# Modulation products in groups of four, x normalised on ScalarE, and the gates' low rank taken with the first head's values

## The chip, the cores and the metric

The kernel runs on one core of a Trainium2 chip. The metric is the device time of one execution in microseconds (us). Three runs of the kernel before took 1918.33, 1924.79 and 1923.61; the median is 1923.61.

## The reference, cut to what matters

The reference is a trunk of two layers over 512 tokens of width 1024: 256 of x and 256 of ctx. A layer modulates its input (a layernorm, times 1 + scale, plus shift), projects it with `w_in` into keys and values, gated linear attention (GLA), a convolution and gates, merges the three branches, and ends with a feed-forward network (FFN) that has a modulation of its own.

```python
mod = (silu_c @ w_ada[l] + b_ada[l])[:, None, :]
sh1, sc1, g1, sh2, sc2, g2 = jnp.split(mod, 6, axis=-1)
...
def _modulate(x, shift, scale):
    return _layernorm(x) * (1.0 + scale) + shift
...
def _mem_parts(pm, p):
    k, v, kg, vg, glr = _split(pm, MEM_SPLITS)
    ...
    gf, gb = _gla_log_gates(glr, p['gla_w_a2'], p['gla_b_a'])
...
def _gla_log_gates(glr, w_a2, b_a):
    z = jnp.einsum('blnr,nrk->nblk', glr.reshape(B, L, 2, GLA_RANK), w_a2) + b_a[:, None, None, :]
    lg = jax.nn.log_sigmoid(z.astype(jnp.float32)) / GLA_TAU
```

Three things in it bear on the change: the first two sixths of the modulation (shift and scale ahead of the mixer), the normalised x of layer 0, and `glr`, the 32 columns of `w_in` (two directions by rank 16) from which the GLA gates are made.

## The kernel before, in words

**Products in three parts.** Each large product of the reference is made of three products in fp32r on TensorE: an operand is split into `hi`, its rounded part (ScalarE, line 98), and `lo`, the rest (VectorE, line 99). `mm3` (line 146) issues hi by hi, hi by lo and lo by hi. Weights come through `wload` (line 102): a tile `raw` of 1024 columns is loaded on SP's queue, split into `whi` and `wlo`, and handed on. There are five `raw`, three `whi` and two `wlo` buffers. `fm` (line 153) makes 128 output features for up to 512 tokens with one `wload` and 24 products. `tm` (line 159) makes token tiles, with the weights as the moving operand.

**Order of the work.** The program is written with the Tile scheduler: an instruction belongs to an engine, the scheduler orders each engine's instructions by priority when the program is built, and it places the waits. The engines then work through their queues in order. `tc.high_priority` moves instructions forward; `wload` uses it with `self.ahead`, which is 30 at the start and 3000 after the keys and values of layer 0. Background work is written as generators, which `step()` advances after each weight group of the main work (`self.bg` for attention and GLA, `ada` for the modulation).

**The start (`run`, line 810).** `silu_c` makes silu(c) for x and ctx as 32 columns (`self.sc`). Four token tiles of x and ctx are loaded in halves of 512 columns, their statistics taken on VectorE (line 824) and completed on GpSimd (`rstd`, lines 91 and 94), and both halves normalised in place on VectorE (line 827). Between the second and the third tile five steps of the generator `ada_head(0)` are run. `layer_consts(0)` follows: it loads the columns of constants, the query and key norms and the rotary table, and makes `rope` with four products on GpSimd (line 241). The rotary table and `rope` are two of the four `t4` tiles, and `rope` is kept.

**`ada_head` (line 254)** computes shift and scale of the mixer in four blocks j of 512 columns. A block has eight products of `self.sc` (the stationary operand, 32 columns) with 512 columns of weights, k = 0 to 7, added up in four column groups of one PSUM tile: product k writes partitions 32g to 32g + 31 with g = k % 4 (line 277). Each product appears in the trace as two records. The weights come in four loads of 1024 columns, two products each, into `t4` tiles (layer 0, even j; line 272), pairs of `qt` tiles (layer 0, odd j; line 269) or `raw` tiles (layer 1). After each load's pair of products the generator yields. After eight, the sum is copied (line 281), transposed and gathered by eight small products with `self.sel` (line 284), and added to the bias (line 285).

**Keys and values of layer 0.** `kv(start)` runs a `tm` with four weight loads. Ahead of the j-th, `start(j)` (line 935) calls `modulate` for the two 128-column units 2j and 2j + 1 of both halves of the tokens (transposes at line 344, two ScalarE instructions at line 352 and one on VectorE at 354 for each unit and half), and then advances `ada_head(0)` by five steps, the next block. Each load is followed by 24 products.

**Layer 1's modulation** is advanced by `step()` within the FFN of layer 0: five steps for each of four blocks, and then two generators `ada_gen` of nine steps (line 290; two `raw` tiles and four products in four column groups per step). The FFN's first three groups are computed in two stages of 256 tokens, the others on 512.

**GLA's low rank.** After the convolution's input, one `fm` over `wglr` (the 32 columns of glr, each direction repeated four times: 128 features) gives `pg` for 512 tokens; line 969 rounds it, and line 970 gives `glrT`, whose rows are rounded values and their rests. `gla_in(hd)` (line 976) then computes a head's keys, queries and values; the values of 256 columns come from two weight loads of 1024 columns and, for each of four token tiles, 24 products 256 wide, evacuated at line 1003. `gla_prep` (line 466), a background generator, uses `glrT` in two products per head (line 479).

Of the kernel before, what the change touches and what calls it, by code (L numbers as in the profile page):

```python
# [52 lines left out]
class Trunk:  # L53
# [48 lines left out]
    def wload(self, src, n=1024, shift=0):  # L102

        nc, tc = self.nc, self.tc
        with tc.high_priority(offset=self.ahead):
            raw = self.T("raw", [128, 1024])
            nc.sync.dma_start(out=raw[:, :n], in_=src)
            hi = self.T("whi", [128, 1152], F32R)[:, shift:shift + n]
            lo = self.T("wlo", [128, 1152], F32R)[:, shift:shift + n]
            self.split(hi, lo, raw[:, :n])  # L110
        return hi, lo

    def wload_hl(self, src):

        nc = self.nc
        with self.tc.high_priority(offset=self.ahead):
            raw = self.T("raw", [128, 1024])
            nc.sync.dma_start(out=raw, in_=src)
            his, los = [], []
            for kk in range(2):  # L120
                hi, lo = self.pair()
                self.split(hi, lo, raw[:, kk * 512:(kk + 1) * 512])
                his.append(hi)
                los.append(lo)
        return his, los
# [128 lines left out]
    def ada_head(self, l, res):  # L254
# [8 lines left out]
        for j in range(4):  # L263
            ps = self.PS("sd")
            for i in range(4):
                if l == 0 and j % 2:
                    raw = [self.T("qt", [128, 512], name="ada") for _ in range(2)]
                    for kk in range(2):
                        nc.sync.dma_start(out=raw[kk], in_=I["w_ada0"][l, j, i][:, kk * 512:(kk + 1) * 512])
                else:  # L270
                    raw = self.T("raw" if l else "t4", [128, 1024], name="ada")
                    nc.sync.dma_start(out=raw, in_=I["w_ada0"][l, j, i])
                    raw = [raw[:, :512], raw[:, 512:]]
                for kk in range(2):
                    k = 2 * i + kk
                    g = k % 4
                    nc.tensor.matmul(ps[32 * g:32 * g + 32, :], self.sc[:, k, :], raw[kk],  # L277
                                     start=(k < 4), stop=(k >= 4))
                yield
            m = self.T("cacc", [128, 512], name="m")  # L280
            nc.vector.tensor_copy(m, ps)
            tr = self.PS("tr", (128, 8))
            for t in range(4):
                nc.tensor.matmul(tr[:, 2 * t:2 * t + 2], m[:, t * 128:(t + 1) * 128], self.sel, start=True, stop=True)
            nc.vector.tensor_tensor(out=mc.rearrange("p (s h k) -> p s h k", s=2, h=2)[:, :, :, 2 * j:2 * j + 2],
                                    in0=tr.rearrange("p (h t s) -> p s h t", h=2, t=2),
                                    in1=b[:, :, :, 2 * j:2 * j + 2], op=ALU.add)
            yield

    def ada_gen(self, l, r, res):  # L290
# [3 lines left out]
        for k in range(KC):  # L294
            for hf in range(2):
                raw = self.T("raw", [128, 1024])
                c0 = (r - 1) * 2048 + hf * 1024
                nc.sync.dma_start(out=raw, in_=I["w_ada"][l, k * 128:(k + 1) * 128, c0:c0 + 1024])
# [511 lines left out]
    def run(self):  # L810
# [4 lines left out]
        self.ada0 = self.ada_head(0, mod)  # L815
        for t in range(4):
            if t == 2:
                for _ in range(5):
                    next(self.ada0)
# [5 lines left out]
            mv, rs = self.stats(st)  # L825
            for n in range(2):
                nc.vector.tensor_scalar(out=x[n], in0=x[n], scalar1=mv[:, 0:1], scalar2=rs, op0=ALU.subtract,  # L827
                                        op1=ALU.mult)
            xn[t] = x
        self.l = 0  # L830
        self.layer_consts(0)
# [17 lines left out]
    def layer(self, l, xn, mod, x0, x1, x2, mgd):  # L849
# [9 lines left out]
        ada = []  # L859
# [75 lines left out]
        def start(j):  # L935
# [3 lines left out]
            for _ in range(5):  # L939
                next(self.ada0, None)  # L940
# [19 lines left out]
        for g in range(ng):  # L960
            if g == NX_GLU:
# [3 lines left out]
        pg = self.PS("mm")  # L965
        self.fm(I["wglr"][l], pg, h)
        self.glrT = self.cpool.tile([128, 512], F32R, tag="glrT", bufs=1, name=self.nm("glrT"))
        gh = self.T("tB", [128, 512], name="glrh")
        nc.scalar.activation(out=gh.bitcast(F32R), in_=pg, func=AF.Copy)
        nc.vector.scalar_tensor_tensor(out=self.glrT, in0=gh, scalar=self.col[:, C_M2:C_M2 + 1], in1=pg,  # L970
                                       op0=ALU.mult, op1=ALU.add)
# [4 lines left out]
        def gla_in(hd):  # L976
# [15 lines left out]
            ws = [self.wload(I["wvg"][l, hd, j], shift=112) for j in range(2)]  # L992
            for t in range(4):
                ps = self.PS("mm", (128, 256))
                for k in range(KC):
                    hi, lo = ws[k // 4]
                    s = slice(k % 4 * 256, (k % 4 + 1) * 256)
# [4 lines left out]
                with self.evac():  # L1002
                    nc.scalar.activation(out=vg[t // 2][:, t % 2, :], in_=ps, func=AF.Copy)
                if t % 2:
                    step()
            me = []
# [193 lines left out]
def pack(x, c, ctx, c_ctx, w_ada, b_ada, w_in, q_norm, k_norm, w_att_o, gla_w_a2, gla_b_a, gla_norm, w_gla_o,  # L1200
# [9 lines left out]
    def tmaj(w, n=512):  # L1210
# [17 lines left out]
    glr = np.concatenate([2048 + 16 * d + np.arange(16) for d in (0, 0, 0, 0, 1, 1, 1, 1)])  # L1228
# [15 lines left out]
        "wglr": fmaj(w_in[:, :, glr])[:, 0], "wq": tmaj(w_in[:, :, 2080:3104]),  # L1244
# [17 lines left out]
```

## Time and profile before

| | |
|---|---|
| median of three runs | 1923.61 us |
| profiled execution | 1923.12 us |
| its span | 1921.1 us |
| busy: PE, PEld | 1837.5, 1498.2 us |
| busy: DVE, ACT, POOL | 1300.9, 866.6, 167.5 us |
| mean granted TensorE clock | 0.986 |

PE is TensorE's products and PEld its weight loads, DVE is VectorE, ACT is ScalarE, POOL is GpSimd, and SPq is the queue on which SyncE issues the loads. The span runs from the first to the last instruction. A row of the timeline has the start, the length, the engine and line, the operation with the tile written and the tiles read, how many instructions were merged into the row, and in brackets the idle time ahead of it and what ended it. A row of groups has the busy time, the mean length in ns and the idle time ahead. The chain is the work that ended last, followed back from the end. Busy time of PE is modelled at its ends, so the distance from one start to the next tells more than a length.

### The profile page before, as it was taken

What the parts mean: (1) busy time and instruction counts of PE and PEld (TensorE: products, weight loads), DVE (VectorE), ACT (ScalarE), POOL (GpSimd) and SP (SyncE); (2) the same over time, 40 slices, a digit from 0 to 9 for tenths busy, and PEclk for the clock granted to TensorE, in tenths of its full rate; (3) what the DMA queues carried; (4) which work ended last, traced back from release to release, by engine and by line L of the source; (5) the groups of instructions that cost most, each with busy time, mean ns of one, the idle gap of its engine ahead of it and who ended that gap; (6) DMA issues with size and microseconds to landing.
All of it is one profiled execution on the core that took longest, in us unless ns stands there. A gap on an engine that the chain in (4) does not pass through costs nothing.

```text
span 1921.1 us, 29251 instructions
## 1 busy us (share of the span) xinstructions
PE 1837.5 (96%) x11300; PEld 1498.2 (78%) x11300; DVE 1300.9 (68%) x2280; ACT 866.6 (45%) x1482; POOL 167.5 (9%) x235
## 2 busy tenths in 40 slices
PE   6999999999999999989999999989999999979998
PEld 2677788677777878867776888877888889969996
DVE  3597999987653445774333457689999777675656
ACT  2445434435733343453222334555455476445442
POOL 1111000012011001100000000031000200110000
PEclk8999999999999999989999999999999999989999
DMA  6421122632374334565466357643233435765663
GB/s 229 163 78 45 56 77 90 215 116 76 104 254 161 100 124 142 190 211 177 161 215 229 121 198 225 220 126 110 86 100 123 149 121 167 235 212 161 191 208 122
DMA packets 90892, 292.30 MB, mean 152 GB/s; under 512 B 10353, under 2 KB 12145, under 8 KB 90753
## 3 DMA queue, kind: packets, MB, share of 16 engines
q1 hardware_dynamic: 90752, 290.43, 46.8%
q8 instruction: 89, 1.46, 0.3%
q14 instruction: 51, 0.41, 0.1%
HBM read 277.77 MB, written 12.62 MB: 151 GB/s over the span
## 4 chain that ended last, share of the span: by engine, by line
PE 79%; DVE 10%; ACT 4%; issue 2%; POOL 2%; DMA 2%; SPq 0%; DVEq 0%; POOLq 0%; ACTq 0%
PE mm L137 66%; DVE acc L674 4%; DVE wlo L99 3%; PE sd L449 2%; PE sd L423 2%; PE sd L277 2%; PE mm L301 2%; PE sd L557 1%; PE sd L610 1%; ACT whi L98 1%; DMA ada<-in_w_ada 1%; PE sd L637 1%; PE tr L444 1%; POOL sg L94 1%; PE tr L344 1%
## 5 line engine op out<-in xcount | busy, mean ns | idle before, releaser
L99 DVE TENSOR_TENSOR wlo<-raw,whi 128x1024 fp32r<-128x1024 f32 x378 | 466.7, 1236 | 317.9 <-PE mm L137 230.9
L137 PE MATMUL mm<-hi,whi 128*128 128x512 f32 (+1 forms) x1920 | 657.5, 343 | 1.1 <-ACT whi L98 0.5
L137 PE MATMUL mm<-hi,wlo 128*128 128x512 f32 (+1 forms) x1920 | 650.5, 339 | 2.5 <-DVE wlo L99 2.3
L137 PE MATMUL mm<-lo,whi 128*128 128x512 f32 (+1 forms) x1920 | 651.4, 340 | 0.8 <-DVE lo L354 0.7
L98 ACT ACTIVATE whi<-raw 128x1024 fp32r<-128x1024 f32 x378 | 400.7, 1061 | 537.3 <-PE mm L137 416.8
L137 PEld LDWEIGHTS mm<-hi,whi 128*128 128x128 f32 x1920 | 364.5, 190 | 64.6 <-issue 12.7
L137 PEld LDWEIGHTS mm<-lo,whi 128*128 128x128 f32 x1920 | 365.2, 190 | 43.3 <-DVE lo L354 3.2
L137 PEld LDWEIGHTS mm<-hi,wlo 128*128 128x128 f32 x1920 | 364.5, 190 | 43.1 <-DVE wlo L99 4.8
L674 DVE SCALAR_TENSOR_TENSOR acc<-y,cols,acc 128x512 f32<-128x512 f32 (+1 forms) x464 | 288.5, 622 | 9.8 <-issue 0.2
L137 PE MATMUL mm<-wlo,hi 128*128 128x512 f32 (+1 forms) x676 | 238.6, 353 | 7.5 <-DVE wlo L99 7.5
L137 PE MATMUL mm<-whi,hi 128*128 128x512 f32 (+1 forms) x676 | 239.6, 356 | 0.6 <-ACT hi L352 0.6
L137 PE MATMUL mm<-whi,lo 128*128 128x512 f32 (+1 forms) x676 | 236.8, 351 | 0.0
L137 PEld LDWEIGHTS mm<-wlo,hi 128*128 128x128 f32 x676 | 127.6, 189 | 32.6 <-DVE wlo L99 9.9
L137 PEld LDWEIGHTS mm<-whi,hi 128*128 128x128 f32 x676 | 127.5, 189 | 22.1 <-issue 2.4
L137 PEld LDWEIGHTS mm<-whi,lo 128*128 128x128 f32 x676 | 127.5, 189 | 20.5 <-issue 2.5
L91 POOL TENSOR_SCALAR sm<-sm 128x1 f32<-128x1 f32 (+1 forms) x38 | 15.9, 418 | 756.9 <-DVE sm L332 664.6
L1036 POOL TENSOR_TENSOR mgp<-mgp,mgold 128x512 f32<-128x512 f32 x24 | 32.3, 1346 | 266.2 <-DVE mgp L1034 230.7
L277 PE MATMUL sd<-ada,sc 128*32 128x512 f32 x128 | 41.4, 703 | 11.8 <-DVE x L827 9.4
L449 PEld LDWEIGHTS sd<-pt,v 128*128 128x128 f32 x320 | 39.9, 191 | 16.0 <-ACT pt L446 12.1
L581 DVE TENSOR_TENSOR X<-X,sums 128x256 f32<-128x256 f32 (+1 forms) x112 | 47.6, 426 | 4.6 <-PE sd L557 3.3
L682 POOL TENSOR_TENSOR csum<-csum,y 128x512 f32<-128x512 f32 (+1 forms) x14 | 18.4, 1313 | 360.9 <-DVE y L674 360.9
L449 PE MATMUL sd<-pt,v 128*128 128x128 f32 x320 | 47.2, 286 | 2.6 <-ACT pt L446 1.1
(227 smaller groups left out, 2033.9 us busy)
## 6 DMA issues: line engine op xcount, KB each, us to landing
raw<-in_wfm SPq DMA_DIRECT2D x112, 512.0 KB
raw<-in_wff SPq DMA_DIRECT2D x94, 512.0 KB
raw<-in_wdown SPq DMA_DIRECT2D x66, 512.0 KB
raw<-in_w_ada SPq DMA_DIRECT2D x64, 512.0 KB
raw<-in_wbr SPq DMA_DIRECT2D x48, 512.0 KB
ada<-in_w_ada SPq DMA_DIRECT2D x24, 512.0 KB
raw<-in_wout SPq DMA_DIRECT2D x24, 512.0 KB
raw<-in_wq SPq DMA_DIRECT2D x16, 512.0 KB
```

The costliest lines, as they stand in the source:

```text
L94: nc.gpsimd.tensor_tensor(out=out, in0=t[:, :n], in1=self.mhalf.to_broadcast([128, n]), op=ALU.pow)
L98: nc.scalar.activation(out=hi, in_=src, func=AF.Copy)
L99: (eng or nc.vector).tensor_tensor(out=lo, in0=src, in1=hi.bitcast(F32), op=ALU.subtract)
L137: i = self.nc.tensor.matmul(*a, **k)
L277: nc.tensor.matmul(ps[32 * g:32 * g + 32, :], self.sc[:, k, :], raw[kk], start=(k < 4), stop=(k >= 4))
L301: nc.tensor.matmul(ps[32 * gg:32 * gg + 32, :], self.sc[:, k, :], raw[:, g * 512:(g + 1) * 512], start=(k == 0), stop=(k == KC - 1))
L344: nc.tensor.transpose(tr[:, kk, t * 128:(t + 1) * 128], xn[t][(k2 + kk) // 4][:, (k2 + kk) % 4 * 128:((k2 + kk) % 4 + 1) * 128], self.ident)
L423: nc.tensor.matmul(ps[:, :nk], qT[:, hh, :], self.kT[:, n, ko:512], start=True, stop=True)
L449: nc.tensor.matmul(po, self.v[:, ko // 128 + c, n * 128:(n + 1) * 128], pt[:, c, :], start=(c == 0), stop=(c == nkc - 1))
L581: nc.vector.tensor_tensor(out=a, in0=a, in1=t, op=ALU.mult)
L674: nc.vector.scalar_tensor_tensor(out=out, in0=win(y, sel, t), scalar=tap(t), in1=acc, op0=ALU.mult, op1=ALU.add)
L1036: nc.gpsimd.tensor_tensor(out=p, in0=p, in1=old, op=ALU.add)
```

## The change

- **`ada_head`.** For layer 0 all loads of a block come first, then its eight products without a yield between, in reverse order of k. For layer 1 a block has two halves of two loads and four products (four column groups), with a yield after each half. A block is one step in layer 0 and three steps in layer 1, in place of five.
- **The start.** All four tiles of x come before the first block. The normalising is done by two ScalarE instructions with scale 1/sigma and bias -mean/sigma, the bias by one small VectorE instruction. `layer_consts(0)` moves from there into `start(2)`, behind the fourth block.
- **Low rank.** The `fm` over `wglr` is gone. Head 0's values are computed with the 32 columns of glr appended, 288 columns in place of 256, from two weight loads of 1152 columns. A second ScalarE instruction per token tile copies the 32 columns, each direction repeated four times, into `low`; four transposes bring it into the layout of the former `pg`, and lines 969 and 970 follow as before, now behind head 0's values.
- **`raw`** is 1152 columns wide in all its uses.

```diff
-            raw = self.T("raw", [128, 1024])
+            raw = self.T("raw", [128, 1152])
...
-            for i in range(4):
...
-                for kk in range(2):
-                    k = 2 * i + kk
+            for n0 in (0,) if l == 0 else (0, 1):
+                parts = []
+                for i in range(4) if l == 0 else range(2 * n0, 2 * n0 + 2):
+                    if l == 0 and j % 2:
+                        for kk in range(2):
+                            raw = self.T("qt", [128, 512], name="ada")
+                            nc.sync.dma_start(out=raw, in_=I["w_ada0"][l, j, i][:, kk * 512:(kk + 1) * 512])
+                            parts.append((2 * i + kk, raw))
+                    else:
+                        raw = self.T("raw" if l else "t4", [128, 1024], name="ada")
+                        nc.sync.dma_start(out=raw, in_=I["w_ada0"][l, j, i])
+                        parts += [(2 * i, raw[:, :512]), (2 * i + 1, raw[:, 512:])]
+                for n, (k, raw) in enumerate(parts[::-1]):
                     g = k % 4
-                    nc.tensor.matmul(ps[32 * g:32 * g + 32, :], self.sc[:, k, :], raw[kk],
-                                     start=(k < 4), stop=(k >= 4))
-                yield
+                    nc.tensor.matmul(ps[32 * g:32 * g + 32, :], self.sc[:, k, :], raw,
+                                     start=(n0 == 0 and n < 4), stop=(l > 0 and n0 == 1 or n >= 4))
+                if l:
+                    yield
...
-        self.ada0 = self.ada_head(0, mod)
         for t in range(4):
-            if t == 2:
-                for _ in range(5):
-                    next(self.ada0)
...
+            nb = self.T("sm", [128, 1])
+            nc.vector.scalar_tensor_tensor(out=nb, in0=mv[:, 0:1], scalar=-1.0, in1=rs, op0=ALU.mult, op1=ALU.mult)
             for n in range(2):
-                nc.vector.tensor_scalar(out=x[n], in0=x[n], scalar1=mv[:, 0:1], scalar2=rs, op0=ALU.subtract,
-                                        op1=ALU.mult)
+                nc.scalar.activation(out=x[n], in_=x[n], func=AF.Identity, scale=rs, bias=nb)
             xn[t] = x
+        self.ada0 = self.ada_head(0, mod)
+        next(self.ada0)
         self.l = 0
-        self.layer_consts(0)
...
-            for _ in range(5):
-                next(self.ada0, None)
+            next(self.ada0, None)
+            if j == 2:
+                self.layer_consts(0)
...
-        pg = self.PS("mm")
-        self.fm(I["wglr"][l], pg, h)
...
+        def low_rank(g):
+
+            tr = self.PS("tr", (128, 4, 128))
+            for t in range(4):
+                nc.tensor.transpose(tr[:, t, :], g[:, t, :], self.ident)
+            pg = tr.rearrange("p t c -> p (t c)")
...
-            ws = [self.wload(I["wvg"][l, hd, j], shift=112) for j in range(2)]
+            n = 256 if hd else 288
+            ws = [self.wload(I["wvg"][l, hd, j] if hd else I["wvg0"][l, j], 4 * n, shift=112 if hd else 0) for j in range(2)]
...
+                    if not hd:
+                        nc.scalar.activation(
+                            out=low[:, t, :].rearrange("p (d r i) -> p d r i", d=2, r=4),
+                            in_=ps[:, 256:288].rearrange("p (d i) -> p d i", d=2).unsqueeze(2).to_broadcast(
+                                [128, 2, 4, 16]), func=AF.Copy)
...
+            if not hd:
+                low_rank(low)
```

More of the change, by code (lines that the diff above doesn't have):

```diff
@@ L116, in wload_hl @@
         with self.tc.high_priority(offset=self.ahead):
-            raw = self.T("raw", [128, 1024])
-            nc.sync.dma_start(out=raw, in_=src)
+            raw = self.T("raw", [128, 1152])
+            nc.sync.dma_start(out=raw[:, :1024], in_=src)
             his, los = [], []
@@ L295, in ada_gen @@
             for hf in range(2):
[L296 removed]
+                raw = self.T("raw", [128, 1152])
                 c0 = (r - 1) * 2048 + hf * 1024
[L298 removed]
+                nc.sync.dma_start(out=raw[:, :1024], in_=I["w_ada"][l, k * 128:(k + 1) * 128, c0:c0 + 1024])
                 for g in range(2):
@@ L963, in layer @@
             glu(g, slice(0, 512), None)
-        pg = self.PS("mm")
-        self.fm(I["wglr"][l], pg, h)
[L967 to L971, printed above, removed]
+        def low_rank(g):
[3 more added lines that the diff above has]
+            pg = tr.rearrange("p t c -> p (t c)")
+            self.glrT = self.cpool.tile([128, 512], F32R, tag="glrT", bufs=1, name=self.nm("glrT"))
+            gh = self.T("tB", [128, 512], name="glrh")
+            nc.scalar.activation(out=gh.bitcast(F32R), in_=pg, func=AF.Copy)
+            nc.vector.scalar_tensor_tensor(out=self.glrT, in0=gh, scalar=self.col[:, C_M2:C_M2 + 1], in1=pg,
+                                           op0=ALU.mult, op1=ALU.add)
         og = [self.T("qt", [128, 512], name="og") for _ in range(ng)]
@@ L1227, in pack @@
     w2 = w2.reshape(L, 4, 128, 128)
-    glr = np.concatenate([2048 + 16 * d + np.arange(16) for d in (0, 0, 0, 0, 1, 1, 1, 1)])
+    vg0 = np.concatenate([w_in[:, :, 1024:1280], w_in[:, :, 2048:2080]], axis=2).reshape(L, 2, 4, 128, 288)
+    vg0 = vg0.transpose(0, 1, 3, 2, 4).reshape(L, 2, 128, 1152)
     cc = np.concatenate([np.broadcast_to(a.reshape(8, 128).T[:, :, None], (128, 8, 16)) for a in (c, c_ctx)], axis=2)
@@ L1243, in pack @@
         "wkv": tmaj(w_in[:, :, 0:512])[:, 0], "wvg": tmaj(w_in[:, :, 1024:2048], 256),
-        "wglr": fmaj(w_in[:, :, glr])[:, 0], "wq": tmaj(w_in[:, :, 2080:3104]),
+        "wvg0": f(vg0), "wq": tmaj(w_in[:, :, 2080:3104]),
         "wbr": f(np.stack([fmaj(w_att_o), fmaj(w_gla_o), fmaj(w_conv_o)], axis=1)),
```

16 lines of the change are left out of this document (5 added, 11 removed).

## Prediction, made before the changed kernel was run

> **What bounds the kernel now.** I read the page first: the busy times, then the chain that ended last by engine.
>
> ```profile
> span 1921.1 us, 29251 instructions
> PE 1837.5 (96%) x11300; PEld 1498.2 (78%) x11300; DVE 1300.9 (68%) x2280; ACT 866.6 (45%) x1482; POOL 167.5 (9%) x235
> PE 79%; DVE 10%; ACT 4%; issue 2%; POOL 2%; DMA 2%; SPq 0%; DVEq 0%; POOLq 0%; ACTq 0%
> ```
>
> TensorE carries 79% of the chain and idles only 1921.1 - 1837.5 = 83.6 us. A product removed from its queue is therefore time removed, unless something else is late there. The median of the runs is 1923.61; the profiled execution took 1923.12, 2.0 of it outside its span, and I work from that one. What a measurement can tell is 0.3%, or 5.8 us.
>
> Next, the first 75 us by stretches of 5 us (length, busy time of PE, PEld, DVE, ACT, POOL, granted clock, DMA share, GB/s).
>
> ```profile
> 0.00:5.00 5.00, 0.00 (x0) 0.00 (x0) 0.44 (x3) 1.70 (x2) 0.90 (x9) 1.00 0.53 162
> 5.00:10.00 5.00, 0.56 (x2) 0.22 (x4) 4.19 (x13) 0.00 (x0) 1.45 (x9) 1.00 1.00 345
> 10.00:15.00 5.00, 4.97 (x16) 0.57 (x12) 1.00 (x2) 0.00 (x0) 0.51 (x1) 1.00 1.04 402
> 20.00:25.00 5.00, 2.05 (x7) 0.69 (x7) 3.87 (x9) 1.11 (x2) 4.07 (x6) 0.50 1.05 416
> 30.00:35.00 5.00, 5.00 (x17) 1.58 (x15) 0.00 (x0) 0.00 (x0) 0.00 (x0) 1.00 0.00 0
> ```
>
> Until about 25 us the loads set the pace, at 402 to 416 GB/s. Five microseconds later nothing is loaded at all, and PE is full with only 17 instructions. The timeline says why (start, duration, engine, line).
>
> ```profile
> 9.44 5.54 PE L277 MATMUL sd<-ada,sc 128*32 128x512 f32 x16 [9.44 <-DVE x L827]
> 19.59 23.18 SPq L272 DMA_DIRECT2D ada<-in_w_ada  x4
> 21.96 1.80 DVE L827 TENSOR_SCALAR x<-x,sm,sm 128x512 f32<-128x512 f32 x2 [0.76 <-POOL sm L94]
> 23.78 1.92 PE L277 MATMUL sd<-ada,sc 128*32 128x512 f32 x4
> 25.64 0.79 PE L137 MATMUL mm<-whi,hi 128*128 128x512 f32 x1
> 72.78 0.39 PE L137 MATMUL mm<-hi,whi 128*128 128x512 f32 x1
> ```
>
> K and V begin at 25.64 and the first product of the next stage is at 72.78, 47.1 us later; in between SP waits 23 us with four modulation loads. The modulation's products stand between those of K and V in pairs (four records are two products). What a pair costs, and what four side by side cost, is read where PE is full:
>
> ```profile
> 927.93 0.39 PE L137 MATMUL mm<-hi,wlo 128*128 128x512 f32 x1
> 928.25 1.05 PE L277 MATMUL sd<-ada,sc 128*32 128x512 f32 x4
> 929.23 0.50 PE L137 MATMUL mm<-hi,whi 128*128 128x512 f32 x1
> ...
> 522.20 0.39 PE L137 MATMUL mm<-hi,wlo 128*128 128x512 f32 x1
> 522.52 1.06 PE L301 MATMUL mm<-raw,sc 128*32 128x512 f32 x8
> 523.51 0.50 PE L479 MATMUL sd<-glrT,w 64*128 64x512 f32 x2
> ```
>
> From one product of L137 to the next is 0.227 when nothing is between (5.21 us for 23 steps, rows under C). Across a pair it is 929.23 - 927.93 = 1.30, so the pair costs 1.07. Across four products in four column groups it is 523.51 - 522.20 = 1.31: the same.
>
> **The change, part by part.**
>
> *A. Start of layer 0.* All of x is now loaded before the first modulation block. By the rates above 0.81 MB arrive by 5 us and 2.54 MB by 10. cc and x are 2.23 MB, so x is complete before 10 us; with the first block 4.33 MB are wanted, and the last 1.79 MB at 402 GB/s put its end at 14.5. The normalising of the last x tile:
>
> ```profile
> 9.35 0.20 DVE L332 BATCH_NORM_AGGREGATE sm<-st 128x2 f32<-128x12 f32 x1
> 10.55 1.00 DVE L827 TENSOR_SCALAR x<-x,sm,sm 128x512 f32<-128x512 f32 x2 [1.00 <-POOL sm L94]
> 822.66 1.52 ACT L782 ACTIVATE xn<-u,sm,sm 128x512 f32<-128x512 f32 x2 [1.31 <-DVE sm L780]
> 17.36 0.56 ACT L352 ACTIVATE hi<-tr,modcol 128x256 fp32r<-128x256 f32 x1 [14.08 <-PE tr L344]
> ```
>
> From the aggregate to the normalising is 1.20, then 1.52 for two halves on ACT (L782 does the same thing later in the kernel) in place of 1.00 on DVE: done at about 13. That is before the block is there, so the dearer engine is hidden; without that cover it costs 0.5. ScalarE is idle here, and the DVE pair at 21.96, beside POOL's rope work, took 1.80. The Trainium skill (ScalarE: Activation LUTs, Rules for kernel authors) says to keep multiplies and adds on VectorE; as to duration the trace agrees, 1.52 against 1.00, and by that rule alone the edit would lose 0.5 us.
>
> The eight products of a block now wait for all its loads. Two quads follow each other. A pair on the slow clock (0.50 in 20 to 25 us) took 1.92, so I take 3.8 and an end at 18.3. From the end of the first block's products (9.44 to 14.98) to the end of the first hi (17.36 + 0.56) was 2.94 us. The first product of K and V comes at 21.2: 4.4 earlier.
>
> Inside the 47.1 us stand 12 pairs, 12 x 1.07 = 12.8. They become three blocks of 1.07 + 0.98 = 2.05 (the second quad starts without the change of shape; 0.98 is 929.23 - 928.25), 6.2 together. That saves 6.7, if the products are there. SP must not be held: cs and rope (both t4 tiles) no longer stand ahead of the third block, whose loads wait for nothing but the first block's products. Each stage wants 2.5 MB, 6.2 us at 402 GB/s, while PE has (47.1 - 6.7) / 4 = 10 us of work per stage. A late block would hold everything behind it on PE; from both sides this part is worth between 0 and 6.7, and I take 6.7 since the load rate is the nearest row. The constants move behind the fourth block: 0.5 MB of loads and POOL's four rope products.
>
> ```profile
> 21.89 3.33 POOL L241 TENSOR_TENSOR rope<-cs,qk 128x256 f32<-128x256 f32 x4
> POOL kr L383 <- ACT kn L361: 45.9, 1, 45.9
> ```
>
> The first user of rope came 45.9 us after POOL was ready for it; that covers the move. A gives 4.4 + 6.7 = 11.1.
>
> *B. Modulation of layer 1*, in layer 0's FFN. Sixteen pairs become eight quads: 8 x 1.07 = 8.6 less. The generator takes 12 steps in place of 20, each of the eight with two raw tiles (1 MB) at once, and SP's queue is moved past accordingly: the later generators' loads come eight steps sooner. The raw tiles are also those of the weights. Once before, a pair was late:
>
> ```profile
> 839.12 1.92 PE L277 MATMUL sd<-ada,sc 128*32 128x512 f32 x4 [2.40 <-DMA ada<-in_w_ada]
> 845.43 0.41 PE L137 MATMUL mm<-lo,whi 128*128 128x256 f32 x1
> 845.64 0.41 PE L137 MATMUL mm<-hi,wlo 128*128 128x256 f32 x1
> ```
>
> I count one more such wait, 2.4, for the doubled demand: 8.6 - 2.4 = 6.2. The ends are no gain at all and 8.6.
>
> The Trainium skill (TensorE: Matmul & The Clock Gate, Packing small matmuls) gives three column tiles a measured speedup of 2.38, so three side by side would take 1.26 of one; an estimate from that page is some 0.25 us more per quad, 3.5 us over the 14 quads that replace pairs here. The trace disagrees, 1.31 across four against 1.30 across two, and the trace decides.
>
> *C. Low rank, once per layer.* 24 products of L137 go; head 0's 96 products become 288 wide instead of 256.
>
> ```profile
> 271.83 0.39 PE L137 MATMUL mm<-lo,whi 128*128 128x512 f32 x1
> 277.04 0.39 PE L137 MATMUL mm<-hi,whi 128*128 128x512 f32 x1
> 290.52 0.39 PE L137 MATMUL mm<-wlo,hi 128*128 128x256 f32 x1 [1.24 <-DVE wlo L99]
> 299.49 0.28 PE L137 MATMUL mm<-wlo,hi 128*128 128x256 f32 x1
> 299.60 0.28 PE L137 MATMUL mm<-whi,lo 128*128 128x256 f32 x1
> 130.98 0.63 PE tr L444 x4
> L99 DVE TENSOR_TENSOR wlo<-raw,whi 128x1024 fp32r<-128x1024 f32 x378 | 466.7, 1236 | 317.9 <-PE mm L137 230.9
> L479 PE MATMUL sd<-glrT,w x16: 468/498/501, 306.8 to 1608.0; 64*128 64x512 f32 x16
> ```
>
> Removed: 24 x 0.227 = 5.4. Added: 96 x 0.11 x 32/256 = 1.3 (bounds 0, if the weight loads set the 0.11, and 1.3), four transposes 0.63, and 1/8 of a 1.24 split, 0.15, where PE waits for wlo at 290.52. That leaves 3.3 per layer, 6.6 for both. The new ACT copies (four small ones) replace a 1024-wide split and lie beside products. glrT is first used at 306.8 (303.5 once 3.3 are gone). Head 0's values then end at 299.7 - 5.4 + 1.3 + 0.15 = 295.8, and some 3 us for two copies, the transposes and the two old steps (an estimate: five steps of 0.4 to 0.8 like those around it) put the new glrT at 299: about 4 us in hand. If the transposes stand in PE's queue ahead of the copies they need, up to 1 us per layer is lost. Wider raw tiles move every tile behind them in SBUF. Per column, products whose split weights start at column 112 (0.11 / 256 = 0.43 ns, head 0) and at column 0 (0.227 / 512 = 0.44 ns) go at one rate, so I take 0; a sign either way is not excluded and is left to what is unseen.
>
> **Sum:** 11.1 + 6.2 + 6.6 = 23.9, and 1923.1 - 23.9 = 1899.
>
> **The rivals.**
>
> *Given back to DVE.* From 82 to 130 us the chain runs over conv accumulations, and DVE is full (4.86 of 5 us, the third busy time).
>
> ```profile
> 104.16 0.76 DVE acc L674
> 105.00:110.00 5.00, 4.73 (x22) 3.58 (x21) 4.86 (x7) 1.14 (x2) 0.00 (x0) 1.00 0.22 55
> ```
>
> If that stretch were set by DVE alone, starting earlier would buy nothing: A is lost, 1923.1 - 12.8 = 1910. Against it: PE idles 0.27 of 5 us at most, and DVE's work there also begins earlier. Chance 0.12.
>
> *Blocks late at the start.* If each block waits on PE for loads or the order puts it ahead of products that could run, the 6.7 goes: 1906. Chance 0.12.
>
> *Quads run as two pairs.* Then A keeps 4.4, B nothing, C 6.6: 1912. Against it stands the row at 522.52. Chance 0.05. This is also the case in which the change doesn't do what it says.
>
> *Slower: raw tiles starve in the FFN.* In layer 1's modulation two of five raw tiles wait together while weights queue behind them. One late quad costs what 839.12 shows: 2.40 idle, 1.92 instead of 1.05, and the next 24 products at 0.21 instead of 0.11, 2.4; together 5.7. All eight: 45.6 - 8.6 more, less A and C (17.7), is +19.3, 1942. It decides from the fifth late quad on: (8.6 + 17.7) / 5.7 = 4.6. For it: the 256-wide steps are short and would load 1.5 MB each. Against it: L301 already takes two raw tiles per step, without a wait in the row at 522.52. Chance 0.07.
>
> **How the numbers follow.** Forecast 0.62, rivals 0.36, something unseen that leaves no change 0.02. The predicted time is the first case, 1899. Upward the range goes through the rivals at 1906, 1910 and 1912, to 1914; downward it takes B at 8.6 (2.4), a warm first block (3.8 - 2.05 = 1.8), C's widening at 0 (2.6) and K and V without the slow first products that 0.79 at 25.64 shows (some 2, an estimate: four of them at 0.79 in place of 0.227), 1890. Faster by over 0.3% is the forecast and the three middle cases, less a little for their spread, 0.86; within 0.3% 0.07; slower 0.07.
>
> **What would show it.** Right: eight records of L277 in one run, 16 per block in layer 0, K and V starting near 21 us and ending near 62, no SP wait of 20 us before 45 us, L277 in layer 1 as groups of about 1.05 us, no glr product group before head 0, first L479 some 14 us earlier than 306.8. Wrong: idle PE "until DMA ada" of several microseconds in front of the blocks, a clock of 0.5 between 820 and 850 longer than now, or a first L479 that moved by less than K and V did.

## The result, and the profile after

| | before | after |
|---|---|---|
| median | 1924.2 us (4 runs, 1918.33 to 1925.39) | 1902.56 us (4 runs, 1899.42 to 1903.13) |
| ratio | | 0.989, 95% interval 0.9867 to 0.9913 |
| profiled execution, its span | 1923.12, 1921.1 us | 1902.89, 1900.8 us |

The kernel is faster by 1.1%; the two profiled executions are 20.2 us apart, where 23.9 were forecast. The page of the changed kernel, in the three lines that were shown of before:

```profile
span 1900.8 us, 29183 instructions
PE 1812.6 (95%) x11260; PEld 1495.6 (79%) x11260; DVE 1297.7 (68%) x2274; ACT 872.1 (46%) x1496; POOL 164.7 (9%) x235
PE 77%; DVE 12%; ACT 4%; POOL 3%; issue 2%; DMA 2%; SPq 0%; DVEq 0%; POOLq 0%; ACTq 0%
```

PE is busy for 24.9 us less, yet the span is only 20.3 shorter: PE idles 88.2 us in place of 83.6, and VectorE's share of the chain rose from 10 to 12%. Where that is, the gain at matching points tells. I take the start of the same ScalarE instruction in both traces; the gain is before's start less after's.

| at (us of before) | gain | what lies between |
|---|---|---|
| 72.78 (first product after K and V) | 11.9 | start of layer 0 |
| 90 to 266 | 7.2 | 4.7 given back at once, then constant |
| 288, behind the old low-rank group | 12.6 | 24 products gone |
| 326 to 683 | 11.1, later 12.0 | wider values of head 0 |
| 1093 | 19.6 | FFN with layer 1's modulation |
| 1402, behind the second group | 24.7 | 24 products gone |
| 1579 (values of a head), 1739 | 25.5, 20.5 | the last GLA heads of layer 1 |

Near 1579 us the instructions no longer stand in the same order: the copy of a head's values (line 1003 of before) comes 25.5 earlier, the next step of the head's own chain (line 539) 21.6.

The start first. Windows of the changed kernel (length, busy time of PE, PEld, DVE, ACT, POOL, granted clock, DMA share, GB/s):

```profile
20.00:25.00 5.00, 4.76 (x19) 4.38 (x20) 0.77 (x3) 1.90 (x5) 0.00 (x0) 1.00 1.04 419
30.00:35.00 5.00, 4.91 (x30) 4.10 (x29) 1.09 (x2) 0.49 (x2) 0.00 (x0) 1.00 0.95 322
70.00:75.00 5.00, 2.41 (x11) 1.67 (x9) 2.29 (x5) 2.73 (x4) 3.19 (x6) 0.99 0.00 0
```

Before, 30 to 35 us held 17 PE instructions and no load; now it holds 30, and 322 GB/s arrive. The last row is new: PE is busy for 2.41 of 5 us. The timeline of the changed kernel around both places:

```profile
15.77 3.64 PE L280 MATMUL sd<-ada,sc 128*32 128x512 f32 x16 [15.77 <-DMA ada<-in_w_ada]
20.24 1.87 PE L288 MATMUL tr<-sel,m 128*128 128x2 f32 x8 [0.83 <-DVE m L285]
21.96 1.95 PE L348 MATMUL tr<-ident,x 128*128 128x128 f32 x8
23.71 0.80 PE L137 MATMUL mm<-whi,hi 128*128 128x512 f32 x1
27.00 1.95 PE L280 MATMUL sd<-ada,sc 128*32 128x512 f32 x16
...
38.42 3.62 SPq L107 DMA_DIRECT2D raw<-in_wfm  x4
51.55 3.64 SPq L107 DMA_DIRECT2D raw<-in_wq  x2
55.23 0.42 SPq L234 DMA_DIRECT2D qk<-in_qknorm  x1
59.23 3.81 POOL L241 TENSOR_TENSOR rope<-cs,qk 128x256 f32<-128x256 f32 x4 [45.35 <-DMA qk<-in_qknorm]
60.91 0.39 PE L137 MATMUL mm<-hi,whi 128*128 128x512 f32 x1
63.07 0.39 ACT L365 ACTIVATE kn<-mm 128x256 f32<-128x256 f32 x1 [2.95 <-POOL rope L241]
68.29 0.43 DVE L377 TENSOR_TENSOR kr<-kr,sm 128x256 f32<-128x256 f32 x1 [4.38 <-POOL kr L391]
72.02 0.39 PE L137 MATMUL mm<-lo,whi 128*128 128x512 f32 x1
74.17 2.35 DVE L99 TENSOR_TENSOR wlo<-raw,whi 128x1024 fp32r<-128x1024 f32 x2
75.44 0.79 PE L137 MATMUL mm<-hi,wlo 128*128 128x512 f32 x1 [3.03 <-DVE wlo L99]
```

Sixteen records of line 280 in one row are eight products side by side, as forecast. K and V begin at 23.71 (21.2 forecast) and the next stage at 60.91 (62 forecast). The rows from 38.42 on are one chain. The load of qk is issued at 55.23, behind two loads of wq: SP stands from 42.04 to 51.55 ahead of them (its longest wait for a `raw` tile, 9.4 us) and then takes 3.64 for the two. POOL had waited 45.35 us for it. `rope` is done at about 63; ScalarE and POOL go on only then. VectorE takes line 377 one by one as POOL delivers, and the splits of the next weights (74.17) stand behind these in VectorE's queue. PE, which needs one, idles from 72.4 to 75.44 and then starts slowly.

Layer 1's modulation, in the groups of 700 to 1000 us, before and then after (busy time, mean ns, idle ahead):

```profile
L277 PE MATMUL sd<-ada,sc 128*32 128x512 f32 x64 | 18.6, 647 | 2.4 <-DMA ada<-in_w_ada 2.4
```
```profile
L280 PE MATMUL sd<-ada,sc 128*32 128x512 f32 x64 | 12.3, 719 | 0.6 <-DMA ada<-in_w_ada 0.5
```

Busy time fell by 6.3 and the wait for loads by 1.9; the gain between 683 and 1093 is 7.6. Not all of that need be the quads: the granted clock over the 30 us at the FFN's start was 0.72 before (820 to 850 us) and 0.83 after (808 to 838). The low rank in layer 0:

```profile
288.83 0.49 PE L972 MATMUL tr<-ident,low 128*128 128x128 f32 x3
290.58 0.33 PE L972 MATMUL tr<-ident,low 128*128 128x128 f32 x1
290.95 0.60 ACT L976 ACTIVATE glrh<-tr 128x512 fp32r<-128x512 f32 x1 [0.42 <-PE tr L972]
294.97 0.50 PE L483 MATMUL sd<-glrT,w 64*128 64x512 f32 x2
```

The first use of `glrT` moved from 306.8 to 294.97, about as much as everything around it (11.8 of 11.1 to 12.6). Nothing waits for it.

### The profile page after: what moved, and what is told of

Its sections match the earlier page's. It is cut to its first block, busy times and chain, and to the rows that moved or that the text cites. A ratio compares the mean times of both kernels' runs of the same rounds, so it can differ in the third digit from the quotient of the medians.

```text
span 1900.8 us, 29183 instructions
## 1 busy us (share of the span) xinstructions
PE 1812.6 (95%) x11260; PEld 1495.6 (79%) x11260; DVE 1297.7 (68%) x2274; ACT 872.1 (46%) x1496; POOL 164.7 (9%) x235
## 4 chain that ended last, share of the span: by engine, by line
PE 77%; DVE 12%; ACT 4%; POOL 3%; issue 2%; DMA 2%; SPq 0%; DVEq 0%; POOLq 0%; ACTq 0%
PE mm L137 65%; DVE wlo L99 3%; DVE acc L678 3%; PE sd L453 2%; PE sd L427 2%; PE mm L305 1%; PE sd L561 1%; PE sd L614 1%; PE sd L641 1%; PE sd L280 1%; DMA ada<-in_w_ada 1%; ACT whi L98 1%; PE tr L448 1%; DVE X L585 1%; DVE X L592 1%
## 5 line engine op out<-in xcount | busy, mean ns | idle before, releaser
L99 DVE TENSOR_TENSOR wlo<-raw,whi 128x1024 fp32r<-128x1024 f32 (+1 forms) x376 | 465.4, 1240 | 303.7 <-PE mm L137 215.4
L137 PE MATMUL mm<-hi,whi 128*128 128x512 f32 (+1 forms) x1904 | 650.2, 342 | 1.3 <-ACT whi L98 0.8
L98 ACT ACTIVATE whi<-raw 128x1024 fp32r<-128x1024 f32 (+1 forms) x376 | 399.2, 1063 | 537.5 <-PE mm L137 386.6
L137 PEld LDWEIGHTS mm<-hi,whi 128*128 128x128 f32 x1904 | 361.0, 190 | 57.8 <-issue 11.9
L137 PE MATMUL mm<-wlo,hi 128*128 128x512 f32 (+2 forms) x676 | 239.9, 355 | 6.8 <-DVE wlo L99 6.8
L137 PE MATMUL mm<-whi,hi 128*128 128x512 f32 (+2 forms) x676 | 241.1, 357 | 1.2 <-ACT hi L356 1.2
L137 PE MATMUL mm<-whi,lo 128*128 128x512 f32 (+2 forms) x676 | 237.6, 353 | 0.0
L543 ACT ACTIVATE kk<-X 128x256 f32<-128x256 f32 x72 | 29.8, 419 | 39.1 <-DVE X L592 38.7
```

Source lines behind the costliest of these rows:

```text
L98: nc.scalar.activation(out=hi, in_=src, func=AF.Copy)
L99: (eng or nc.vector).tensor_tensor(out=lo, in0=src, in1=hi.bitcast(F32), op=ALU.subtract)
L137: i = self.nc.tensor.matmul(*a, **k)
L543: nc.scalar.activation(out=cap(out[s], 0, [[2 * lev, nb], [lev, 2], [1, lev]]), in_=cap(X[s], W, [[2 * lev, nb], [2 * W + lev, 2], [1, lev ...
```

## The experiments

The theory to begin with: the start wins some 12 us, and 4.7 of it go because qk, whose tile is an `h1` tile and is loaded late, holds `rope`. The rivals put the loss on the low rank or on the wider `raw` tiles. All times below are medians beside runs of the kernel before on the same chip (1922.1 to 1923.9).

| kernel | median us | ratio to before, 95% |
|---|---|---|
| e1_qk_own | 1897.22 | 0.9862 (0.9836 to 0.9888) |
| e2_layer1_quads | 1917.48 | 0.9959 (0.9945 to 0.9974) |
| e3_low_rank | 1913.71 | 0.9947 (0.9929 to 0.9966) |
| e4_wide_raw | 1924.54 | 1.0000 (0.9984 to 1.0017) |
| e5_start | 1919.14 | 0.9978 (0.9961 to 0.9995) |
| e6_norm_dve | 1900.72 | 0.9870 (0.9850 to 0.9890) |
| e8_pairs | 1902.47 | 0.9883 (0.9867 to 0.9899) |
| e9_low_rank0 | 1895.54 | 0.9843 (0.9826 to 0.9859) |
| e10_consts_only | 1922.26 | 0.9995 (0.9982 to 1.0008) |
| e11_x_first | 1918.33 | 0.9984 (0.9971 to 0.9996) |
| e12_bridge | 1895.86 | 0.9861 (0.9846 to 0.9876) |
| e13_group_consts | 1907.38 | 0.9927 (0.9906 to 0.9948) |

**e1_qk_own.** The changed kernel with a place of its own for qk.

```diff
-        qk = self.T("h1", [128, 2, 128], name="qk")
+        qk = self.T("h1" if l else "S", [128, 2, 128], name="qk")
```

> The changed kernel with one edit: in layer 0 the query and key norms (qk) are loaded into a tile of the S group, which is free, and not into one of the h1 group, whose six tiles the modulation uses. Theory (the constants came late): after K and V the changed kernel loses 4.7 us, because VectorE's split of the next weights stands behind the key's rotation, which waits for rope, which waits for qk, loaded at 55.2. Then qk is loaded right behind the fourth block, near 33 us, the 3.0 us wait for wlo near 75 us is gone with the slow products behind it, and the time is about 4.7 below the changed kernel: 1898. Rival (VectorE sets that stretch whatever comes earlier): the wait stays or comes back within the next 50 us and the time is 1902 to 1903.

The timeline of this kernel, and its window from 70 to 75 us:

```profile
32.63 0.45 SPq L234 DMA_DIRECT2D qk<-in_qknorm  x1
39.86 3.80 POOL L241 TENSOR_TENSOR rope<-cs,qk 128x256 f32<-128x256 f32 x4 [25.29 <-PE tr L288]
```
```profile
70.00:75.00 5.00, 5.00 (x25) 4.09 (x24) 3.79 (x6) 1.43 (x2) 0.00 (x0) 1.00 0.55 173
```

qk goes out 22.6 us earlier, `rope` starts 19.4 us earlier, and PE is full where it stood still. The gain is 12.4 from 90 to 266 us instead of 7.2, and 25.0 at 1760 instead of 20.5. The late load of qk is shown to be the cause.

**e2_layer1_quads, e3_low_rank, e4_wide_raw: one part alone on the kernel before.** The first holds a load until the next one is there and issues the four products together (layer 1 only); the second is the low rank with `raw` at 1152 columns; the third is that width alone.

```diff
+                if l and i % 2 == 0:
+                    held = raw
+                    continue
```
```diff
-            raw = self.T("raw", [128, 1024])
+            raw = self.T("raw", [128, 1152])
```

> The kernel before with the second part alone: layer 1's modulation in quads (all eight products of a block in two steps), layer 0 as before. Theory (a quad costs what a pair costs): the stretch from the end of layer 0's second residual to its end is 7.6 shorter, as the changed kernel's was, and the time is 1924.2 - 7.6 = 1916.6. Rival (the gain there came from loads that moved, not from the products): less than 3 us, 1921 or more.

> The kernel before with the low rank alone: head 0's values 288 wide, no product group for the 32 columns, raw tiles of 1152; modulation and start as before. Theory: 4.9 in layer 0 and 4.2 in layer 1, 9.1 in all, and the loss of about 3 in layer 1's later heads comes along if it belongs to this part: 1915 without that loss, 1918 with it. Rival (the removed products were all there is, 3.3 a layer as predicted): 1917.6, with 3.3 at head 1 of layer 0.

> The kernel before with raw tiles of 1152 columns and nothing else; only the first 1024 are used, so that every tile behind them lies 2560 bytes further on in each partition. Theory (an address costs nothing): the time of the kernel before within 2 us, 1924, with the distance of full-rate products unchanged at 0.227. Rival (the new places of the tiles gave part of the gain): 2 to 10 us faster or slower, with another distance between products.

The quads alone win 7.0 in the FFN (from -2.35 at 683 us to 4.7 at 1104), where the changed kernel wins 7.6. The small loss ahead of that is in a stretch in which PE's instructions stand in the same order as before; its cause was not found. The low rank alone wins 6.5 in layer 0 (2.5 to 9.0), and in layer 1 it goes from 8.8 to 14.2 at the group, to 15.7 for the values at 1579 and back to 9.7 at 1750. So the late loss of the changed kernel belongs to the low rank in layer 1, and not to its start. The width alone is worth nothing: up to 683 us all starts agree with before within 0.45 us. Behind that its trace wins 3.4 in the FFN, with the program of before and a granted clock of 0.89 over the same 30 us. So what one trace shows of the FFN's start is uncertain by about that much. From 683 to 1093 us the six traces with pairs in layer 1, before among them, win between 0 and 3.4 us on before (mean 1.7), the eight with quads between 6.6 and 10.6 (mean 8.2). The quads are thus worth some 6.5 us, an estimate from these two means.

**e5_start: the start alone.** The kernel before with the changed start, layer 1's modulation and the low rank as they were.

> The kernel before with the start of layer 0 alone changed: all of x first, normalised on ACT, the modulation blocks of layer 0 as eight products, the constants behind the fourth block. Modulation of layer 1 and the low rank stay as they were. Theory (what the start wins, some 12 us by the end of K and V, is given back by 4.7 because the load of qk comes late, on the start's own account): some 12 us ahead at the first product after K and V, a wait of 2 to 4 us for a split of weights within the 15 us behind it, 7 us ahead from 90 us on, and 1923.5 - 7 = 1916.5. Rival (the 4.7 come from the low rank or the quads of layer 1, whose tiles share SBUF with the start): no such wait, 11 to 12 us ahead to the end, 1912.

Its trace is 11.95 ahead at the first product after K and V (60.83), waits 2.97 for a split at 75.30, and is 7.3 ahead at 90 and 7.2 at 266: the loss is the start's own. The end was not as expected: the median of ten runs is only 4.8 better. The profiled execution, with a span of 1913.2, is one of the shorter ones and ends 8 ahead, so its trace does not show where the others lose. The four runs above 1921 us have a mean granted clock of 0.984 or 0.985, the other six 0.986 to 0.990; why it differs was not found.

**e6_norm_dve.** x normalised on VectorE in the changed kernel.

```diff
-                nc.scalar.activation(out=x[n], in_=x[n], func=AF.Identity, scale=rs, bias=nb)
+                nc.vector.tensor_scalar(out=x[n], in0=x[n], scalar1=mv[:, 0:1], scalar2=rs, op0=ALU.subtract,
+                                        op1=ALU.mult)
```

> The changed kernel with x normalised on DVE as before (no extra scalar for the bias), all else as changed. Theory (the normalising is finished before the first block's loads are there, so its engine costs nothing): first block of products at 15.8 as in the changed kernel, the same time within 1 us, 1902.6. Rival (ACT's longer way, 1.5 for 1.0, and the extra step on the bias lie on the path): first products and all behind them 0.5 to 1 us earlier, 1901.8. Rival (DVE's pair is slowed by POOL beside it): 0.5 to 1 us later.

The first block starts at 15.60 (15.77 in the changed kernel) and the gain at 90 us is 7.0 (7.2). The engine of the normalising makes no difference that can be seen, in the trace or in the time.

**e8_pairs.** The changed kernel with layer 0's blocks 1 to 3 written as pairs again.

```diff
+            for i in range(4) if l == 0 and j else ():
...
+                yield
...
-            next(self.ada0, None)
+            for _ in range(5):
+                next(self.ada0, None)
```

> The changed kernel, with blocks 1 to 3 of layer 0's modulation again in pairs that stand between the products of K and V (block 0 and all else as changed). Products next to each other are worth 12 x 1.07 - 3 x 1.93 = 7.0 in that stage by the rows: the first product after K and V moves from 60.9 to about 68. Theory (behind it the changed kernel waits for rope, ready at about 63, and so for qk's load): rope is then in time, the 4.7 us of waiting behind the stage go, and 7.0 - 4.7 = 2.3 us are lost in all: 1905. If the load of qk moves along with the pairs, the wait stays and all 7.0 are lost: 1909.5. Rival (pairs are hidden by the loads anyway): first product after K and V at 61, 1902.6.

The theory missed, and the rival's numbers came for another reason than the one it gave. The next stage begins at 61.15, not at 68, and the time is that of the changed kernel. The pairs are not hidden by loads; the scheduler put most of them side by side itself:

```profile
15.63 3.64 PE L294 MATMUL sd<-ada,sc 128*32 128x512 f32 x16 [15.63 <-DMA ada<-in_w_ada]
19.07 1.12 PE L277 MATMUL sd<-ada,sc 128*32 128x512 f32 x2
20.12 1.05 PE L302 MATMUL tr<-sel,m 128*128 128x2 f32 x8
21.03 1.12 PE L362 MATMUL tr<-ident,x 128*128 128x128 f32 x8
22.08 1.90 PE L277 MATMUL sd<-ada,sc 128*32 128x512 f32 x10
24.35 1.05 PE L277 MATMUL sd<-ada,sc 128*32 128x512 f32 x2
```

A row of ten records is five products in 1.90, a lone product costs 1.05. What counts is in how many groups the products stand on PE. I then thought that late loads had torn them apart in the kernel before, and tested that with the next two.

**e10_consts_only, e11_x_first.** The kernel before with only the constants moved, and with only x first.

```diff
-        self.layer_consts(0)
...
+            if j == 2:
+                self.layer_consts(0)
```

> The kernel before with one edit: layer 0's constants (qk, cs, rope) move from the front behind the fourth block; x, the pairs and all else as before. Theory (what tore the pairs of layer 0 apart was late loads, held by the t4 tiles of cs and rope; the grouping in the code is not needed, as the version with pairs again showed): K and V begin at 25.6 as before, no load of SP waits 20 us, the pairs of a block come side by side, and the stage behind K and V begins some 6.5 us earlier than 72.8, at 66; then rope is late and 3 to 5 us of it go again: 1921. Rival (the grouping or x first is what shortens the stage): 72 to 73, and a loss behind it where rope comes late: 1923 to 1928.

> The kernel before with one edit: all four x tiles are loaded and normalised (on DVE as before) ahead of the first modulation block, whose pairs stay pairs; the constants stay in front of the blocks behind it. Theory (x first moves the first block's end and no more): K and V begin about 2 us earlier than 25.6, the loads of the third block still wait for the tiles of cs and rope, the stage behind K and V begins at about 71, rope is in time, and the gain of 2 stays: 1921.5. Rival (x first is what brings the loads in time): the stage behind K and V begins at 64 or earlier, 1914.

The timeline of the first:

```profile
18.64 2.26 SPq L272 DMA_DIRECT2D ada<-in_w_ada  x4
...
28.65 8.18 SPq L269 DMA_DIRECT2D ada<-in_w_ada  x6
...
26.70 1.92 PE L277 MATMUL sd<-ada,sc 128*32 128x512 f32 x2
29.58 1.04 PE L277 MATMUL sd<-ada,sc 128*32 128x512 f32 x2
31.45 1.05 PE L277 MATMUL sd<-ada,sc 128*32 128x512 f32 x4
```

No load holds SP for 23 us any more, and still the groups stand apart, since PE's order is fixed when the program is built. K and V take 47.5 us (25.55 to 73.03), as before, and the time is unchanged. That theory fell. With x first alone K and V begin at 23.77 and take 47.15; of the 1.9 us 1.4 are left at 683 us. Its time, 1918.33, is below the 1921.5 expected; the trace wins another 2.9 in the FFN, as that of e4 does with the program of before.

The stage of K and V, taken apart by the distance from one start to the next in the timeline, shows what did it:

| kernel | K, V begin | length | groups | modulation | K, V products | other |
|---|---|---|---|---|---|---|
| before | 25.64 | 47.14 | 14 | 14.42 | 26.83 | 5.89 |
| e10_consts_only | 25.55 | 47.48 | 14 | 14.62 | 27.26 | 5.60 |
| e11_x_first | 23.77 | 47.15 | 14 | 14.38 | 26.88 | 5.89 |
| after | 23.71 | 37.20 | 3 | 5.58 | 24.81 | 6.81 |
| e8_pairs | 23.91 | 37.24 | 6 | 7.59 | 24.04 | 5.61 |
| e13_group_consts | 19.88 | 37.44 | 3 | 5.56 | 25.67 | 6.21 |

The 14 groups hold one, two or three products each, 22 in all. Each group costs about one microsecond, whether it holds one, two or four products: 14.42 / 14 = 1.03, and 5.58 / 6 quads = 0.93. Of e8's blocks two more groups lie ahead of K and V (19.07 and 22.08).

**e13_group_consts.** Grouping and the move of the constants, with x in its old order (two tiles ahead of the first block, two behind) and the low rank as before. Grouping without that move was not tried: `rope` would keep a `t4` tile of which a block needs all four at once.

> The kernel before with the modulation's products grouped (layer 0 in eights, layer 1 in fours) and the constants behind the fourth block; x in its old order, two tiles ahead of the first block and two behind, normalised on DVE; low rank as before. Theory (the grouping is what shortens the stage of K and V, x first only moves its start by 2 us): K and V begin at 25 to 26, the next stage begins some 37 to 38 us later, at 63; of the 10 us some 3 to 5 go again where rope is late; layer 1's modulation gives 7 to 8 in the FFN: 1923.5 - 6 - 7.5 = 1910. Rival (without x first the blocks' loads are late and the blocks hold everything behind them): idle PE ahead of blocks until their loads land, the next stage at 70 or later, 1916 or more.

The timeline of this kernel:

```profile
12.11 3.64 PE L280 MATMUL sd<-ada,sc 128*32 128x512 f32 x16 [12.11 <-DMA ada<-in_w_ada]
17.68 1.05 PE L288 MATMUL tr<-sel,m 128*128 128x2 f32 x8 [1.93 <-DVE m L285]
19.88 2.13 PE L137 MATMUL mm<-whi,hi 128*128 128x512 f32 x4
```

The stage has its 37.4 us, as the theory said. But K and V begin at 19.88, where 25 to 26 were expected, and the next stage at 57.32, 3.6 ahead of the changed kernel: with two tiles of x ahead of it the first block has its loads at 12.11 and not at 15.77. So x first, which wins 1.9 in the old kernel, loses at this place beside the grouping. Not all of the 3.6 is its own: from the first small product to K and V it is 2.20 us here and 3.47 in the changed kernel, where they run at half the rate. Here too some 3 us go back where `rope` is late: the gain is 15.5 at the end of K and V and 12.2 at 87 us.

**e9_low_rank0.** The version of e1 with the low rank joined in layer 0 alone.

```diff
+        if l:
+            pg = self.PS("mm")
+            self.fm(I["wglr"][l], pg, h)
...
-            n = 256 if hd else 288
+            lr = l == 0 and hd == 0
+            n = 288 if lr else 256
```

> The changed kernel with qk in a tile of its own in layer 0, and with the low rank joined to head 0's values in layer 0 alone: layer 1 has its own group of 24 products again. Theory (in layer 1 the joined low rank wins 5.4 at the group, and gives 4 to 6 back in the last two heads, where the order that comes out leaves TensorE fewer products to put beside the heads' chain): the gain stands at about 25 us after 1071, stays at 25 within 1 us to the end, and PE waits for ACT's kk at no place after 1600; 1898, which is what the joined version has. Rival (the late loss comes from the start or from layer 1's quads): 25 at 1400, 20 at 1750, 1903.

What PE waits for between 1480 and 1720 us (us in total, times, longest; the rows that bear on the heads), after, and then this kernel:

```profile
...
PE sd L561 <- ACT kk L543: 5.1, 4, 1.4
PE tr L653 <- ACT on L647: 2.5, 4, 0.7
PE sd L698 <- POOL csum L686: 1.9, 1, 1.9
```
```profile
...
PE tr L653 <- ACT on L647: 2.9, 6, 0.7
PE sd L698 <- POOL csum L686: 2.9, 1, 2.9
```

The wait for kk is gone, and PE's instructions in layer 1 stand in the order of the kernel before. The gain is 25.4 at 1350 us, 25.5 at 1579 and 26.5 at 1760. In e1, with the joined low rank, it goes 24.4, 31.4 (values; 27.4 for the chain of the head), 25.0. So in layer 1 the joined low rank wins 5.4 and gives as much back in the last two heads. That the order there leaves fewer products beside the chain of the heads fits the wait, but was not tried by itself. The timed medians of the two (1895.54 and 1897.22) can't be told apart; against the changed kernel (0.9867 to 0.9913) e9, at 0.9826 to 0.9859, is faster.

**e12_bridge.** e9 with block 1 in pairs, so that its first product stands where PE waits for the sum to be copied.

> The version with qk in a tile of its own and the low rank joined in layer 0 alone, and besides block 1 of layer 0's modulation in pairs, so that its first pair stands in TensorE's queue right behind block 0, where TensorE otherwise waits 0.8 us for the sum to be copied; blocks 2 and 3 stay eight products side by side. Theory (that wait puts TensorE back to half its rate for some 7 us; with the pair in between it stays at the full rate, and the torn block 1 costs 3 us of the 4 to 5 that this saves): the eight small products of the gathering take about 1.05 instead of 1.87, the transposes 1.1 instead of 1.95, and the stage behind K and V begins at 59 to 59.8 in place of 61.5; 1.5 to 2.5 us less in all, 1893.5. Rival (the half rate comes with the clock's own window and not with the wait): transposes at 1.9 as before, the stage behind K and V at 63 to 64, 1898.

```profile
15.62 3.25 PE L294 MATMUL sd<-ada,sc 128*32 128x512 f32 x16 [15.62 <-DMA ada<-in_w_ada]
18.71 1.02 PE L277 MATMUL sd<-ada,sc 128*32 128x512 f32 x2
19.72 1.05 PE L302 MATMUL tr<-sel,m 128*128 128x2 f32 x8
20.63 1.12 PE L362 MATMUL tr<-ident,x 128*128 128x128 f32 x8
...
23.52 0.50 PE L137 MATMUL mm<-whi,hi 128*128 128x512 f32 x1
```

In this timeline the small products take 1.05 and 1.12, and the next stage begins at 59.96 (61.5 in e9): 1.5 us in the trace, which the times don't show (1895.86). For these rows the reason given does not hold, however. In e1 the same wait of 0.84 stands there and the same rows take 1.05 and 1.12; in e13 the wait is 1.93 and the first of them takes 1.05. So the wait alone doesn't decide at which rate they run. What follows them differs, though. In e1:

```profile
20.92 1.05 PE L288 MATMUL tr<-sel,m 128*128 128x2 f32 x8 [0.84 <-DVE m L285]
21.83 1.12 PE L348 MATMUL tr<-ident,x 128*128 128x128 f32 x8
23.12 0.63 PE L137 MATMUL mm<-whi,hi 128*128 128x512 f32 x1 [0.17 <-ACT hi L356]
23.55 0.63 PE L137 MATMUL mm<-wlo,hi 128*128 128x512 f32 x1
```

The first products of K and V are 0.43 apart there, about twice the distance of later ones, and the granted clock reads 0.50 from 24 to 26 us. In e12 and in e8, the two kernels with a product in that wait, they run at full rate; in the twelve other traces they start at about half. That a product in the wait keeps up the rate of what follows fits this, but two traces don't show it.

## Why the prediction was right, and where its steps were not

The direction and the places held, and the end came 3.7 us above the forecast, inside its range. That the sum came so near is in part luck: 4.7 and 2.4 were lost against the terms, and 0.8, 1.4 and 1.5 won. Its terms and what the two profiled executions show:

| term | forecast | measured |
|---|---|---|
| start, to the end of K and V | 11.1 | 11.9 |
| then, to 90 us | 0 | -4.7 |
| modulation of layer 1 | 6.2 | 7.6 |
| low rank, layer 0 | 3.3 | 4.8 |
| low rank, layer 1 | 3.3 | 0.9 |
| sum | 23.9 | 20.5 |

**The step that failed** is "The first user of rope came 45.9 us after POOL was ready for it; that covers the move". The figure is slack of POOL. What had to be covered was a load: the move put qk behind the fourth block in SP's order, on an `h1` tile, and SP then stood with the loads of wq until 55.2. POOL's wait for rope's operands came out as 45.35 us in its turn, and the cover was gone. e1 shows it: with qk loaded early all 12 us stay. The measured price of the step is the 4.7 us of the table.

**A came out right, up to the end of K and V, by two errors.** The start of K and V was forecast 4.4 earlier and came 1.9 earlier: the first block's loads were there at 15.77 (forecast 14.5), and behind it the small products and transposes ran at half their rate (1.87 and 1.95, against 1.05 and 1.12 in e12), where the forecast took a chain of 2.94 from before. The stage itself was forecast 6.7 shorter and came 9.9 shorter. The forecast counted 12 pairs; in the trace 14 groups stand in this stage, seven of them with a single product, and a single product costs as much as a pair (1.05 for the row at 24.35 in e8, and for the pair at 31.45 in e10). The modulation went from 14.42 to 5.58 us, which is 8.8 of the 9.9; the other 1.1 lies in the products of K and V and what stands between them, part of which ran at half rate in both kernels. The credit for x first was wrong as well: beside the grouping K and V begin 3.8 us later than without it (e13), 1.3 of which is the rate of the small products.

**B** was cut by 2.4 for one more wait on a load. The waits fell from 2.4 to 0.5 instead. Ten groups took the place of 16, not eight, as two of the eight quads were split (846.33 and 849.34, 854.84 and 856.73 in the trace after); with the wait it makes 6.3 + 1.9 = 8.2 by the two rows, of which 7.6 arrive. The estimate over all traces, 6.5, is nearer to the forecast than either; the clock at the FFN's start, which the forecast names as a sign but not as a term, can account for the rest.

**C** is right per group: 5.4 removed, and 1.4 for all that was added (12.55 to 11.13 us of gain from 288 to 326 us) against 1.3 + 0.63 + 0.15 = 2.1 forecast for the widening, the transposes and the wider split. Layer 0 then gets back 0.9 by 683 us, for which the runs show no cause. Layer 1 gives nearly all of it back in the last heads; the forecast had no term for what comes after the group.

**The normalising** was forecast hidden, and e6 agrees. The rule of the Trainium skill (ScalarE: Activation LUTs, Rules for kernel authors) to keep multiplies and adds on VectorE, by which 0.5 us would have been lost, holds for the instruction (1.52 against 1.00) and costs nothing at this place. It ran from 10.23 to 15.98 (forecast: done at about 13), past the first block's loads at 15.77; what hid it were that block's products.

**The rivals.** Nothing was given back to VectorE from 87 to 130 us: the gain is 7.2 at the one end and 7.5 at the other. No block waited for loads but the first. The quads ran as quads (1.07 for four products at 844 us). The raw tiles did not starve.

## What to carry to other kernels

Cover is counted for each instruction of a moved step and on each queue: its loads have a place in a queue and a tile to wait for, and a number of idle microseconds on the engine that uses them says nothing of that. Products that cost the same in a group of one and a group of four are counted in groups, in the order in which they come to stand on the engine; how the source is written is only one of the things that decide this order. Where part of a change takes products away from the side of a latency-bound chain, look at the end of that chain before booking the gain.

## What the runs showed of the hardware

- The start varies with the same order of instructions: e3_low_rank has the order of before on PE up to the old low-rank group, and K and V begin at 23.96 in place of 25.64. Of these 1.7 us, 1.0 is the start of the first block (8.44 against 9.44) and 0.7 its length (4.86 against 5.54). The trace of e4 agrees with before within 0.45 us up to the FFN; at the FFN's start it gains 3 to 4 us. Both are places where PE had idled. The Trainium skill (TensorE: Matmul & The Clock Gate, What's actually happening) says that the gate looks at a window that runs freely, so that the moment of the change depends on where in it the first product falls. The traces agree in that the same rows take 1.87 and 1.95 in the changed kernel and 1.05 and 1.12 in e1; they disagree with the 3.4 us of that section, since half the rate lasted from 15.77 to about 27 us in the changed kernel, over one pause of 0.83 us.
- The column of the granted clock reads 1.00 from 20 to 25 us of the changed kernel, while its small products and transposes take 1.87 and 1.95. There the distance between starts tells the rate, and the column does not. From 24 to 26 us it reads 1.00 in the changed kernel and 0.50 in e1, while the products of K and V are 0.43 apart in both.
